# Part of a one-core mixer's weights split into high and low halves ahead of time and kept in DRAM, other remainders moved from GpSimd to VectorE, and the q, k norm multiplied from PSUM

## The chip, the cores and the metric

The kernel runs on one core of a Trainium2 chip. The metric is the device time of one execution in microseconds; the time before is the median of three runs. A core has TensorE (PE, with weight loads listed as PEld), VectorE (DVE), ScalarE (ACT), GpSimd (POOL) and SyncE (SP). DVE and ACT can read PSUM, the memory into which PE accumulates, in eight banks of 128x512 f32. SP here only issues DMAs, in the order of the program; POOL issues those DMAs that add to their target. Each engine works off its own instructions in order.

## The reference

One layer of a streaming encoder on x of 1024 x 1024, f32, in three residual steps:

```
h  = rmsnorm(x);  z = h @ w_in         # q, f, i, g (HGRN), q, k, v (band attention), two gates
oa = hgrn2(q, f, i, g)                 # 4 heads of 128, a recurrence over chunks of 64
ob = band_attention(q, k, v)           # 8 heads of 64, own chunk and the 8 before it
       # q and k go through head_rms first: t * rsqrt(mean(t*t over 64) + eps) * gain
x += (sigmoid(gate_a) * (oa @ w_branch_a) + sigmoid(gate_b) * (ob @ w_branch_b)) @ w_out
x += (silu(h2 @ w_gate) * (h2 @ w_up)) @ w_down          # h2 = rmsnorm(x)
x += sigmoid(h3 @ w_ple_gate) * (p @ w_ple_proj)         # h3 = rmsnorm(x)
```

## The kernel before

*Products in three passes.* Each f32 operand a is split into hi = a rounded to the type that PE multiplies at full rate, and lo = a - hi. A product is hi*hi + hi*lo + lo*hi (`gemm`). The split is a cast (hi) and a subtraction (lo, "the remainder"). Of a weight, ACT makes hi and mostly POOL makes lo.

*Order of the work.* The program is one long Python routine (`run`) that emits instructions; every engine keeps the emitted order (`order`, line 71). The stages are:

1. **units** (line 967): the first norm, the projections whose weights are combined before use (gates, HGRN's q, f, g), as twelve jobs (`JOBS`) of seven products each (`strassen`). While one job's products run, a generator `side` prepares the next job's weights: sums on DVE, casts on ACT, remainders on DVE and POOL (`strassen_weights`). Results go to DRAM.
2. **the HGRN heads 0 to 3** (`hgrn_mix`): chains of small DVE products, each level feeding small matmuls. They are woven (`weave`) with a stream of large products, `fill`: two gates (`gate_first`), v (`attn_v`), and the first part of q, k (`attn_in`). Each item of the stream is six 128x512 matmuls. Loads of each head's operands are issued by SP in the same emitted order (`head_load`, `head_late`, `near`).
3. **the attention** (`attention`): 32 steps of scores, softmax, transposes and products with v; between them, two items per step of the rest of `attn_in` and then of `branch_a` (oa @ w_branch_a). At steps 18, 19, 19 and 20 (`SPLITS`), `split_in` casts HGRN's output on ACT and makes its remainder on POOL.
4. **branches, out_proj, FFN, ple**: the rest, which the change does not touch but for one line.

*Weights of stages 2 and 3.* The list `worder` holds pieces of 128x1024 f32 (512 KB): two gates, four of v, eight of q and k (four for the first half of the heads, four for the second), then the branches'. `fetch` (line 166) takes the next one: it issues the load into one of two raw buffers (`RAW`) and puts a generator `cast` in the list `later`. `tick` advances everything in `later` by one step; `ticked` calls it after each item of the stream. So two to three items after the load, ACT casts the piece into one of four ring buffers (`RING`), and POOL makes the remainder right behind it. `got` hands out finished pieces.

*The norm of q and k* (`qk_norm`, line 652) is a generator in `later` too, one for each of 16 results of 128x512 in PSUM. In its first step it copies the result to SBUF (ACT in the heads, DVE in the attention) and squares it in PSUM; in the second DVE sums the squares, POOL takes the power -0.5 and multiplies the copy; three ticks later SP stores it. The attention loads it back (`qk_load`).

*POOL's other work there:* DMAs that add blocks of the weights of w_out and w_ffn_down in DRAM (`dma_sums`), issued at every odd step and at each pair of tiles of `branch_a`.

In the profile, line 73 stands for every instruction of DVE, ACT and POOL that goes through the ordering helper (`Pinned`), line 104 for matmuls, line 107 for transposes, line 99 for SP's DMAs. Tiles: `wr` raw weight, `wh` and `wl` its halves, `whi` and `wlo` halves in the units, `s` a 128x1024 slot, `m` a small tile, `pm` a PSUM bank, `t` a 128x512 scratch tile, `d` a block in DRAM, `in_...` an input.

Of the kernel before, what the change touches and what calls it, by code (L numbers as in the profile page):

```python
# [11 lines left out]
F32R = mybir.dt.float32r  # L12
U8 = mybir.dt.uint8
U32 = mybir.dt.uint32
AF = mybir.ActivationFunctionType
ALU = mybir.AluOpType
AX = mybir.AxisListType

P = 128
T = 1024  # L20
D = 1024
# [9 lines left out]
SLOTS = 32  # L31
LATE = 8
FIRST = 5
GROUPS = ((0, 1), (2,), (3,), (4,), (5,), (6, 7))
RING = 4
RAW = 2
# [9 lines left out]
def f32(ap):  # L46
    return ap.bitcast(F32)
# [28 lines left out]
class Trunk:  # L76
    def __init__(self, tc, d, out):
        self.tc, self.nc, self.d, self.out = tc, tc.nc, d, out
        self.V = Pinned(self, self.nc.vector, "dve")
        self.A = Pinned(self, self.nc.scalar, "act")  # L80
        self.G = Pinned(self, self.nc.gpsimd, "pool")
        self.n = self.turn = 0
        self.queue, self.calls = None, 0
        self.later = []
        self.by_turns = self.pinned = False
        self.ahead = 2
        self.done = set()
        self.prev = {}
# [77 lines left out]
    def fetch(self):  # L166

        if self.wnext < len(self.worder):
            hi, lo, raw, ap = self.unit()
            c = slice(0, ap.shape[1])  # L170
            self.load(raw[:, c], ap[:, c])

            def cast():
                yield
                yield
                self.A.copy(hi[:, c], raw[:, c])
                self.G.tensor_tensor(lo[:, c], raw[:, c], f32(hi[:, c]), ALU.subtract)
                self.wready.append((hi, lo))

            self.later.append(cast())  # L180

# [8 lines left out]
            yield got  # L190

    def got(self, n=1):
        while len(self.wready) < n:
            assert self.later
            self.tick()
        got, self.wready = self.wready[:n], self.wready[n:]
        return got

    def lazy(self, ws):
        for _ in range(4):  # L200
# [450 lines left out]

    def qk_norm(self, k, ps):

        late = self.stacks
        qk = self.small(HALF, tag="qk" if late else "bias", shape=(P, HALF if late else 640))[:, :HALF]
        (self.V.tensor_copy if late else self.A.copy)(qk, ps)
        self.A.activation(ps, ps, AF.Square)
        yield
        ss = self.small(8)
        heads = lambda t: t.rearrange("p (a d) -> p a d", d=64)  # L660
        self.V.tensor_reduce(ss, heads(ps[:, :]), axis=AX.X, op=ALU.add)
        b = k % 8
        self.V.tensor_scalar(ss, ss, 1.0 / 64, self.epsv[:, b:b + 1], ALU.mult, ALU.add)
        self.G.tensor_tensor(ss, ss, self.mhalf[:, 0:8], ALU.pow)
        self.G.tensor_tensor(heads(qk), heads(qk), ss[:, :].unsqueeze(2).to_broadcast([P, 8, 64]), ALU.mult)
        yield
        yield
        yield
        self.store(self.qk_at(k), qk)
# [199 lines left out]
    def split_in(self, raw):  # L869

        hi = self.slot(F32R)
        self.A.copy(hi, f32(raw[:, :]))
        self.G.tensor_tensor(raw, f32(raw[:, :]), f32(hi[:, :]), ALU.subtract)
        return hi, raw

    def split_half(self, src, half):
# [84 lines left out]
    def units(self, outs):  # L961

        V, A = self.V, self.A
        h0, h1 = slice(0, HALF), slice(HALF, T)
        self.gd = [self.spill() for _ in range(2 * KC)]
        self.gh = [self.spill() for _ in range(4)]
        self.vd = [self.spill() for _ in range(4)]
        self.hd = [[] for _ in range(4)]
        self.kept = []
        self.t32, self.t1, self.xs = [], [], []  # L970

        ws = self.weights(4, ahead=0)
        for k in range(4):
            xe = self.slot()
            if k < 2:
                xo = self.slot()
                self.mix_load(k, xe, [xo[:, :HALF], xo[:, HALF:]], xo)
            else:
                self.mix_load(k, xe, [self.stmp(), self.stmp()])
        self.strassen_load()  # L980
        side = chain(*[self.mix_sums(k) for k in range(4)])

        def rest():
            more = self.units_first()
            next(more)
            yield
            yield from self.mix_last()
            for i in (2, 3, 0, 1):
                self.head_out(0, *head, i // 2, i % 2, outs[i])
                yield  # L990
            yield from more

        for blks in ((0, 1), (2,), (3,), (4,), (5,), (6,), (7,)):
            pss = []
            for j, _ in enumerate(self.tokens(ws, blks, pss)):
                if blks[0] == 0 and j == 3:
                    self.norm_sums()
                next(side, None)
            if blks[0] == 4:
                self.strassen_load()  # L1000
            for b, ps in zip(blks, pss):
                t = self.stmp()
                A.activation(t, ps, AF.Copy, scale=self.r[:, b:b + 1])
                to = self.vd[b // 2][:, b % 2 * HALF:b % 2 * HALF + HALF]
                if b >= 4:
                    to = bass.AP(to.tensor, to.offset + (TURN - 1) * T, [[TURN * T, P // TURN], [-T, TURN], [1, HALF]])
                self.store(to, t)
            if blks[0] == 0:
                self.norm_rows()
            if blks[0] == 4:  # L1010
                drain(side)
                head = self.slot(), self.slot()
                side = rest()
        drain(side)
        u, t = self.u, self.t32
        cut = lambda pair, h: [x[:, h] for x in pair]
        four = range(4)
        self.sops = [
            [cut(u[2 * k + 1], h1) for k in four], [cut(t[k], h1) for k in four],
            [cut(self.t1[k // 2], slice(k % 2 * HALF, k % 2 * HALF + HALF)) for k in four], [cut(t[k], h0) for k in four],  # L1020
            [cut(u[2 * k], h1) for k in four], [cut(u[2 * k + 1], h0) for k in four], [cut(u[2 * k], h0) for k in four]]
        pack = self.head_pack(0, *head)
        for n, (kind, i) in enumerate(JOBS):

            def side():
                more = self.strassen_weights() if n + 1 < len(JOBS) else self.mix_first()
                next(more, None)
                if n + 2 < len(JOBS):
                    self.strassen_load()
                yield  # L1030
                for _ in more:
                    next(pack, None)
                    yield
                drain(pack)

            if kind == "head":
                q, f = self.slot(), self.slot()
                done = lambda c, half, ps: self.head_out(i, q, f, c, half, ps)
            elif kind == "gate":
                done = lambda c, half, ps: self.gate_done(self.gd[i + c], half, ps, AF.Sigmoid)  # L1040
            else:
                done = lambda c, half, ps: self.gate_done(self.gh[i + c], half, ps, AF.Silu)
            self.strassen(done, side(), early=n == 0)
            if kind == "head":
                pack = self.head_pack(i, q, f)
        self.gate_keep()
        for k in range(4):
            hi, lo = self.u[2 * k + 1]
            c = C_MIX + 2 * k + 1
            g = self.cols[:, c:c + 1]  # L1050
            A.activation(hi[:, h0], self.xb[k], AF.Copy, scale=g)
            V.scalar_tensor_tensor(lo[:, h0], self.xb[k], g, f32(hi[:, h0]), ALU.mult, ALU.subtract)
        self.A.activation(self.warm, self.warm, AF.Sigmoid)

    def units_first(self):
# [24 lines left out]
        self.wrest(G, cut(a12, h1), r2[:, h1])  # L1080
        yield
        self.sready = (a11, cut(s21, h0), cut(s21, h1), s3, cut(a12, h0), cut(a12, h1), s4)

    def mix_first(self):
        self.fetch()
# [61 lines left out]
    def branches(self):  # L1147
# [4 lines left out]
        drain(self.feed)  # L1152
        while self.later:
            self.tick()
        for dd in range(4):
            (w,) = self.weights()
            next(self.adds, None)
# [933 lines left out]
    def run(self):  # L2091
# [17 lines left out]
        with ExitStack() as es:  # L2109
            self.cp = es.enter_context(tc.tile_pool(name="const", bufs=1))  # L2110
            self.wp = es.enter_context(tc.tile_pool(name="weights", bufs=RING))
            self.rp = es.enter_context(tc.tile_pool(name="raw", bufs=RAW))
            self.dp = es.enter_context(tc.tile_pool(name="spill", bufs=4 * KC + 11 * STEPS + 56, space=bass.MemoryType.DRAM))
            self.sp = es.enter_context(tc.tile_pool(name="slots", bufs=SLOTS))
            self.tp = Small(tc, es, SMALL)
            self.pp = es.enter_context(tc.tile_pool(name="psum", bufs=8, space=PS))
# [60 lines left out]
class Small:  # L2177
# [5 lines left out]
    def tile(self, shape, dt, tag, name):  # L2183
        return self.pools[tag].tile(shape, dt, tag=tag, name=name)


def drain(stream):
    while True:
        try:
            next(stream)  # L2190
        except StopIteration as e:
            return e.value
# [125 lines left out]
```

## Time and profile before

| what | us |
|---|---|
| median of three runs (1553.53 to 1553.84) | 1553.71 |
| the profiled execution | 1554.34 |
| its span, first to last instruction | 1552.5 |
| PE busy (98%) | 1518.9 |
| DVE busy (72%) | 1122.6 |
| ACT busy (43%) | 665.0 |
| POOL busy (44%) | 683.2 |

The units take the span up to about 306 us, the heads with their stream to about 470, the attention to about 680; from there to the end it is branches, output, FFN and the last step. The mean granted clock of PE is 0.993 of full speed. In the views, "idle before <-" names what released an engine from a wait; a row of the timeline gives start, duration, engine, line, operation, output<-inputs and count.

### The profile page before, as it was taken

How to read it: one execution, taken by the hardware profiler on the slowest of the kernel's cores; microseconds unless marked ns; L12 is line 12 of the kernel's file. 1: busy time of each engine (PE TensorE's matmuls, PEld its weight loads, DVE VectorE, ACT ScalarE, POOL GpSimd, SP SyncE). 2: the span in 40 equal slices, each digit the busy share in tenths (PEclk: the TensorE clock that was granted, in tenths of full speed). 3: DMA queues.
4: the chain of work that ended last, by engine and by line, in shares of the span. 5: the costliest groups of instructions: out<-in, count | busy, mean ns of one | idle time of the engine just before them, and what ended most of it. 6: DMA issues, size and time to landing. Idle time of an engine off the chain costs nothing.

```text
span 1552.5 us, 20777 instructions
## 1 busy us (share of the span) xinstructions
PE 1518.9 (98%) x7680; PEld 1251.0 (81%) x7680; DVE 1122.6 (72%) x1594; ACT 665.0 (43%) x1119; POOL 683.2 (44%) x383
## 2 busy tenths in 40 slices
PE   8999999999898998999999999999999999999998
PEld 6888888878786886888888888888888888888886
DVE  5776777476776766746998877777777767756668
ACT  6633333344335665741557322222222234446552
POOL 4233333320235426237221666665555544545546
PEclk9999999999999998999999999999999999999999
DMA  5543444466537768558245234443333288875425
GB/s 202 193 169 103 143 143 156 176 239 213 181 118 249 178 188 256 139 154 259 90 163 216 97 115 125 128 125 113 107 103 104 94 310 302 288 273 186 129 95 203
DMA packets 101940, 264.95 MB, mean 171 GB/s; under 512 B 10576, under 2 KB 15440, under 8 KB 101328
## 3 DMA queue, kind: packets, MB, share of 16 engines
q1 hardware_dynamic: 95296, 247.90, 46.1%
q0 software_dynamic: 6400, 15.73, 6.1%
q8 instruction: 60, 0.98, 0.3%
q14 instruction: 40, 0.33, 0.1%
q10 hardware_dynamic: 144, 0.02, 0.0%
HBM read 197.28 MB, written 97.78 MB: 190 GB/s over the span
## 4 chain that ended last, share of the span: by engine, by line
PE 83%; DVE 8%; DMA 3%; issue 2%; POOL 2%; ACT 2%; SPq 0%; DVEq 0%; POOLq 0%; ACTq 0%
PE pm L104 81%; DVE s L73 6%; PE pm L107 3%; POOL s L73 1%; DMA wr<-in_qk 1%; ACT s L73 1%; DVE m L73 1%; DMA wr<-in_bb 1%; POOL wl L73 0%; DVE wl L152 0%; ACT wh L144 0%; DMA s<-in_x 0%; POOL wl L152 0%; DMA wr<-in_ow 0%; DMA m<-d 0%
## 5 line engine op out<-in xcount | busy, mean ns | idle before, releaser
L104 PE MATMUL pm<-s,whi 128*128 128x512 f32 x1904 | 586.4, 389 | 0.0
L104 PE MATMUL pm<-s,wh 128*128 128x512 f32 (+1 forms) x1456 | 455.1, 393 | 13.9 <-POOL s L73 6.8
L104 PEld LDWEIGHTS pm<-s,whi 128*128 128x128 f32 x1904 | 357.4, 188 | 74.2
L104 PE MATMUL pm<-s,wlo 128*128 128x512 f32 x952 | 370.6, 389 | 0.5 <-DVE wlo L73 0.5
L73 DVE TENSOR_TENSOR s<-s,s 128x512 f32<-128x512 f32 (+3 forms) x240 | 296.5, 1265 | 58.7 <-ACT s L73 42.5
L104 PEld LDWEIGHTS pm<-s,wh 128*128 128x128 f32 x1456 | 271.9, 189 | 72.7 <-POOL s L73 7.6
L104 PE MATMUL pm<-s,wl 128*128 128x512 f32 (+1 forms) x728 | 284.3, 391 | 0.5 <-POOL wl L152 0.5
L152 POOL TENSOR_TENSOR wl<-wr,wh 128x1024 fp32r<-128x1024 f32 (+3 forms) x71 | 177.0, 2496 | 218.7 <-ACT wh L144 215.3
L73 DVE TENSOR_TENSOR t<-pm,t 128x512 f32<-128x512 f32 x168 | 115.7, 689 | 147.3 <-PE pm L104 124.9
L104 PEld LDWEIGHTS pm<-s,wlo 128*128 128x128 f32 x952 | 178.7, 188 | 38.1 <-DVE wlo L73 1.2
L104 PE MATMUL pm<-wh,s 128*128 128x512 f32 x512 | 181.7, 410 | 0.0
L73 POOL TENSOR_TENSOR wlo<-q,whi 128x512 fp32r<-128x512 f32 x66 | 105.1, 1593 | 164.2 <-ACT whi L73 87.8
L73 POOL TENSOR_TENSOR wlo<-wr,whi 128x1024 fp32r<-128x1024 f32 (+1 forms) x67 | 139.8, 2093 | 68.4 <-ACT whi L73 59.3
L104 PEld LDWEIGHTS pm<-s,wl 128*128 128x128 f32 x728 | 137.5, 189 | 29.7 <-POOL wl L152 1.2
L144 ACT CAST wh<-wr 128x1024 fp32r<-128x1024 f32 (+2 forms) x82 | 81.2, 992 | 154.6 <-PE pm L104 41.2
L73 ACT CAST s<-s 128x1024 fp32r<-128x1024 f32 (+1 forms) x104 | 98.7, 970 | 61.7 <-DMA s<-d 27.0
L73 ACT CAST whi<-q 128x512 fp32r<-128x512 f32 (+1 forms) x99 | 75.0, 758 | 107.0 <-PE pm L104 87.1
L73 POOL TENSOR_TENSOR s<-t,rb 128x512 f32<-128x512 f32 x44 | 71.2, 1619 | 99.3 <-ACT t L73 99.3
L104 PEld LDWEIGHTS pm<-wh,s 128*128 128x128 f32 x512 | 97.5, 190 | 19.0
L104 PE MATMUL pm<-wl,s 128*128 128x512 f32 x256 | 101.0, 394 | 0.0
L73 POOL TENSOR_TENSOR wl<-wr,wh 128x1024 fp32r<-128x1024 f32 x25 | 61.0, 2444 | 90.3 <-ACT wh L73 83.5
L73 ACT ACTIVATE t<-s 128x512 f32<-128x512 f32 x44 | 27.8, 632 | 158.6 <-DVE s L73 154.6
(149 smaller groups left out, 1809.3 us busy)
## 6 DMA issues: line engine op xcount, KB each, us to landing
s<-d SPq DMA_DIRECT2D x81, 512.0 KB, 6.5
d<-s SPq DMA_DIRECT2D x87, 256.0 KB, 2.3
wr<-d SPq DMA_DIRECT2D x36, 512.0 KB, 3.4
d<-s SPq DMA_DIRECT2D x30, 512.0 KB, 4.7
d<-t SPq DMA_DIRECT2D x54, 256.0 KB, 2.1
wr<-in_sz SPq DMA_DIRECT2D x24, 512.0 KB, 6.1
wr<-in_sg SPq DMA_DIRECT2D x22, 512.0 KB, 4.0
wr<-in_su SPq DMA_DIRECT2D x22, 512.0 KB, 4.2
```

The source lines that it names most:

```text
L73: return lambda *a, **k: self.trunk.order(op(*a, **k), self.key)
L104: return self.order(self.nc.tensor.matmul(*a, **k))
L107: return self.order(self.nc.tensor.transpose(*a, **k))
L144: self.nc.scalar.copy(hi[:, c], raw[:, c])
L152: rest.tensor_tensor(lo[:, c], raw[:, c], f32(hi[:, c]), ALU.subtract)
```

## The change

- **Pieces prepared in the units.** In jobs 1, 2, 9 and 10, `side` runs a new generator `presplit` for two pieces each: the four of v and the first four of q, k. It loads the piece into a slot, ACT casts it, POOL makes the remainder, and both halves are stored to DRAM (two blocks of 512 KB). `fetch` then loads both halves of such a piece straight into ring buffers, with no cast, and marks it ready at once.
- **Other remainders.** The two gates, the last four of q, k and the pieces of the branches that `fetch` takes are still cast by ACT, but DVE makes the remainder, one tick after the cast. A list `order_w` with ready marks takes the place of `wready` until `branches` begins. `split_in` also leaves its remainder to DVE, at the next tick.
- **The norm.** `qk_norm` no longer copies the result: ACT squares from PSUM into SBUF, DVE sums, POOL takes the power, and a tick later DVE multiplies straight from PSUM into the tile that is stored. The PSUM bank is held until then.
- The pool of DRAM blocks grows by 16.

```diff
+PRE = {1: (0, 1), 2: (2, 3), 9: (4, 5), 10: (6, 7)}
...
     def fetch(self):
         if self.wnext < len(self.worder):
+            parts = self.parts.get(self.wnext)
+            if parts:
+                self.wnext += 1
+                w = self.wtiles(D)
+                for t, src in zip(w, parts):
+                    self.load(f32(t[:, :]), src)
+                self.order_w.append([w, True])
+                return
             hi, lo, raw, ap = self.unit()
...
                 yield
                 yield
                 self.A.copy(hi[:, c], raw[:, c])
-                self.G.tensor_tensor(lo[:, c], raw[:, c], f32(hi[:, c]), ALU.subtract)
-                self.wready.append((hi, lo))
+                yield
+                self.V.tensor_tensor(lo[:, c], raw[:, c], f32(hi[:, c]), ALU.subtract)
+                entry[1] = True
+
+            entry = [(hi, lo), False]
+            self.order_w.append(entry)
...
     def got(self, n=1):
-        while len(self.wready) < n:
-            assert self.later
+        while not all(ready for _, ready in self.order_w[:n]):
             self.tick()
-        got, self.wready = self.wready[:n], self.wready[n:]
-        return got
+        got, self.order_w = self.order_w[:n], self.order_w[n:]
...
     def qk_norm(self, k, ps):
-        late = self.stacks
-        qk = self.small(HALF, tag="qk" if late else "bias", shape=(P, HALF if late else 640))[:, :HALF]
-        (self.V.tensor_copy if late else self.A.copy)(qk, ps)
-        self.A.activation(ps, ps, AF.Square)
+        tile = lambda: self.small(HALF, tag="qk" if self.stacks else "bias", shape=(P, HALF if self.stacks else 640))[:, :HALF]
+        heads = lambda t: t.rearrange("p (a d) -> p a d", d=64)
+        sq = tile()
+        self.A.activation(sq, ps, AF.Square)
         yield
         ss = self.small(8)
-        heads = lambda t: t.rearrange("p (a d) -> p a d", d=64)
-        self.V.tensor_reduce(ss, heads(ps[:, :]), axis=AX.X, op=ALU.add)
         b = k % 8
+        self.V.tensor_reduce(ss, heads(sq), axis=AX.X, op=ALU.add)
         self.V.tensor_scalar(ss, ss, 1.0 / 64, self.epsv[:, b:b + 1], ALU.mult, ALU.add)
         self.G.tensor_tensor(ss, ss, self.mhalf[:, 0:8], ALU.pow)
-        self.G.tensor_tensor(heads(qk), heads(qk), ss[:, :].unsqueeze(2).to_broadcast([P, 8, 64]), ALU.mult)
-        yield
+        yield
+        qk = tile()
+        self.V.tensor_tensor(heads(qk), heads(ps[:, :]), ss[:, :].unsqueeze(2).to_broadcast([P, 8, 64]), ALU.mult)
         yield
         yield
         self.store(self.qk_at(k), qk)
...
     def split_in(self, raw):
         hi = self.slot(F32R)
         self.A.copy(hi, f32(raw[:, :]))
-        self.G.tensor_tensor(raw, f32(raw[:, :]), f32(hi[:, :]), ALU.subtract)
+        def rest():
+            self.V.tensor_tensor(raw, f32(raw[:, :]), f32(hi[:, :]), ALU.subtract)
+            yield
+        self.later.append(rest())
         return hi, raw
...
+                pre = [self.presplit(j) for j in PRE.get(n, ())]
                 yield
                 for _ in more:
                     next(pack, None)
+                    for p in pre:
+                        next(p, None)
                     yield
                 drain(pack)
+                for p in pre:
+                    drain(p)
...
+    def presplit(self, j):
+        k = 6 + len(FIRSTS) + j
+        raw, hi = self.slot(F32R), self.slot(F32R)
+        self.load(f32(raw[:, :]), self.worder[k])
+        yield
+        yield
+        self.A.copy(hi, f32(raw[:, :]))
+        self.G.tensor_tensor(raw, f32(raw[:, :]), f32(hi[:, :]), ALU.subtract)
+        yield
+        self.parts[k] = [self.spill() for _ in range(2)]
+        for to, t in zip(self.parts[k], (hi, raw)):
+            self.store(to, f32(t[:, :]))
...
     def branches(self):
         while self.later:
             self.tick()
+        self.wready = [w for w, _ in self.order_w]
```

More of the change, by code (lines that the diff above doesn't have):

```diff
@@ L84, in __init__ @@
         self.later = []
+        self.parts, self.order_w = {}, []
         self.by_turns = self.pinned = False
@@ L192, in got @@
     def got(self, n=1):
-        while len(self.wready) < n:
-            assert self.later
+        while not all(ready for _, ready in self.order_w[:n]):
             self.tick()
-        got, self.wready = self.wready[:n], self.wready[n:]
-        return got
+        got, self.order_w = self.order_w[:n], self.order_w[n:]
+        assert len(got) == n
+        return [w for w, _ in got]
     def lazy(self, ws):
@@ L2112, in run @@
             self.rp = es.enter_context(tc.tile_pool(name="raw", bufs=RAW))
-            self.dp = es.enter_context(tc.tile_pool(name="spill", bufs=4 * KC + 11 * STEPS + 56, space=bass.MemoryType.DRAM))
+            self.dp = es.enter_context(tc.tile_pool(name="spill", bufs=4 * KC + 11 * STEPS + 72, space=bass.MemoryType.DRAM))
             self.sp = es.enter_context(tc.tile_pool(name="slots", bufs=SLOTS))
```

## The prediction

> **What bounds the kernel now.** I read the page's head first: TensorE (PE) is busy 98% of the span.
>
> ```profile
> span 1552.5 us, 20777 instructions
> PE 1518.9 (98%) x7680; PEld 1251.0 (81%) x7680; DVE 1122.6 (72%) x1594; ACT 665.0 (43%) x1119; POOL 683.2 (44%) x383
> ```
>
> So a change that removes no matmul can win only what PE idles, 1552.5 - 1518.9 = 33.6 us, and what it runs at a lower clock. The second view, busy time by stretch (width first, then PE, PEld, DVE, ACT, POOL, the granted clock, DMA share, GB/s), says where that is. The first row is a units job (`strassen`) that gets new work; the six others are the mixer.
>
> ```profile
> 98.00:117.00 19.00, 19.00 (x86) 15.73 (x85) 14.16 (x20) 7.52 (x12) 8.17 (x4) 1.00 0.70 250
> 300.00:395.00 95.00, 94.11 (x578) 78.93 (x577) 63.74 (x110) 36.86 (x77) 13.09 (x8) 1.00 0.65 222
> 395.00:422.00 27.00, 22.50 (x151) 18.47 (x150) 24.11 (x33) 12.51 (x28) 10.00 (x5) 0.94 0.71 209
> 422.00:475.00 53.00, 51.31 (x343) 43.45 (x342) 35.99 (x73) 17.16 (x40) 17.76 (x14) 1.00 0.32 103
> 475.00:510.00 35.00, 30.40 (x177) 22.20 (x178) 22.06 (x69) 22.88 (x66) 20.82 (x13) 0.95 0.85 267
> 510.00:578.00 68.00, 67.73 (x585) 55.91 (x583) 48.78 (x177) 46.03 (x114) 21.26 (x18) 1.00 0.72 191
> 578.00:612.00 34.00, 27.20 (x140) 19.38 (x136) 19.72 (x47) 19.75 (x55) 23.41 (x15) 0.85 0.81 241
> ```
>
> PE idles 0.89, 4.50, 1.69, 4.60, 0.27 and 6.80 us in the six mixer rows, 18.75 us together, and three of them show a clock below 1. The same view on the long holes and what follows them:
>
> ```profile
> 345.60:346.70 1.10, 0.41 (x2) 0.00 (x0) 1.10 (x2) 0.00 (x0) 0.53 (x1) 1.00 0.00 0
> 399.90:402.10 2.20, 0.76 (x4) 0.29 (x2) 2.20 (x3) 0.67 (x2) 0.95 (x1) 1.00 0.27 28
> 414.60:418.10 3.50, 0.48 (x3) 0.08 (x2) 3.50 (x5) 0.00 (x0) 2.18 (x1) 1.00 1.09 278
> 418.60:422.00 3.40, 3.40 (x17) 2.81 (x15) 2.35 (x5) 0.20 (x1) 0.00 (x0) 0.50 0.95 302
> 483.80:486.60 2.80, 0.42 (x2) 0.00 (x0) 1.69 (x4) 2.80 (x11) 2.33 (x1) 1.00 1.07 345
> 486.90:490.20 3.30, 3.30 (x12) 2.27 (x12) 2.25 (x9) 1.82 (x8) 2.38 (x1) 0.50 1.08 284
> 497.30:499.00 1.70, 0.42 (x3) 0.23 (x3) 1.70 (x5) 1.18 (x3) 0.00 (x0) 1.00 1.05 236
> 589.60:592.50 2.90, 0.46 (x3) 0.03 (x2) 1.51 (x3) 2.15 (x8) 2.90 (x3) 1.00 1.03 420
> 592.70:596.00 3.30, 3.30 (x12) 2.11 (x12) 3.30 (x3) 0.48 (x1) 2.03 (x1) 0.50 1.08 325
> 598.20:603.00 4.80, 0.52 (x2) 0.19 (x1) 4.69 (x7) 3.15 (x8) 3.40 (x3) 0.99 0.52 126
> 603.00:609.70 6.70, 6.62 (x31) 4.81 (x32) 2.60 (x8) 1.16 (x4) 6.54 (x7) 0.50 0.47 110
> ```
>
> The holes cost 0.69, 1.44, 3.02, 2.38, 1.28, 2.44 and 4.28 us of PE. Four are followed by a stretch at clock 0.50 (3.4, 3.3, 3.3, 6.7 us), in which half the time is lost: 1.7, 1.65, 1.65, 3.35. Grouped: **heads** (before 422) 0.69 + 1.44 + 3.02 + 1.7 = 6.85; **weights of q, k** (483 to 499) 2.38 + 1.65 + 1.28 = 5.3; **splits** (589 to 610) 2.44 + 1.65 + 4.28 + 3.35 = 11.7. Together 23.9 us; the 1.69 us between 422 and 475 and the 0.27 after 510 come in pieces well below these, and I leave them as they are.
>
> The third view, the timeline, names the cause. Heads:
>
> ```profile
> 395.93 1.28 DVE L73 TENSOR_TENSOR s<-s,s 128x512 f32<-128x512 f32 x2
> 398.46 2.39 POOL L73 TENSOR_TENSOR wl<-wr,wh 128x1024 fp32r<-128x1024 f32 x1 [2.94 <-PE pm L104]
> 398.83 3.17 DVE L73 TENSOR_TENSOR s<-s,s 128x512 f32<-128x512 f32 x2
> ...
> 412.08 4.70 POOL L73 TENSOR_TENSOR wl<-wr,wh 128x1024 fp32r<-128x1024 f32 x2 [3.83 <-ACT wh L73]
> 412.12 2.40 DVE L73 TENSOR_TENSOR s<-s 128x32 f32<-128x32 f32 x1
> ```
>
> The same pair of VectorE (DVE) products takes 1.28 us alone and 3.17 beside POOL's remainder of a weight; a small 128x32 product takes 2.40 beside the next two. DVE stands still while POOL works on SBUF, and PE, which waits for these products, stands with it.
>
> Weights of q and k, and splits:
>
> ```profile
> 479.09 0.29 DVE L73 TENSOR_SCALAR s<-s,m 128x128 f32<-128x128 f32 x1
> ...
> 483.02 1.05 ACT L73 CAST wh<-wr 128x1024 fp32r<-128x1024 f32 x1 [3.37 <-DMA wr<-in_qk]
> ...
> 485.24 1.34 DVE L73 TENSOR_SCALAR s<-s,m 128x128 f32<-128x128 f32 x1
> 486.52 3.21 SPq L99 DMA_DIRECT2D wr<-in_qk  x2
> ...
> 588.98 1.07 POOL L73 DMA_DIRECT2D d<-in_wq  x1
> 589.58 5.14 POOL L73 TENSOR_TENSOR s<-s,s 128x1024 fp32r<-128x1024 f32 x2
> 591.31 3.58 DVE L73 TENSOR_SCALAR s<-s,m 128x256 f32<-128x256 f32 x1
> 599.60 1.06 POOL L73 DMA_DIRECT2D d<-in_wq  x1 [4.87 <-DMA m<-d]
> ```
>
> At 483 there are two causes: ACT stood 3.37 us for a weight that had not landed, and then a softmax scaling took 1.34 us beside POOL's remainder instead of the 0.29 of the step before. At 589 and 598 PE waits directly for POOL's remainders of the HGRN output (`split_in`), the last of which stood 4.87 us behind an accumulating DMA.
>
> **The change, part by part.** Prices of what replaces POOL's work:
>
> ```profile
> L73 DVE TENSOR_TENSOR s<-s,s 128x1024 fp32r<-128x1024 f32 x2 | 2.4, 1222 | 2.5 <-ACT s L73 2.5
> L73 POOL TENSOR_TENSOR m<-m,mhalf 128x8 f32<-128x8 f32 x16 | 27.4, 1712 | 58.2 <-DVE m L73 48.7 <-DMA m<-in_bias 9.4
> L73 POOL TENSOR_TENSOR m<-m,m 128x512 f32<-128x512 f32 x16 | 16.9, 1056 | 1.3
> L73 DVE COPY m<-pm 128x512 f32<-128x512 f32 x12 | 7.9, 680 | 0.0
> L73 DVE TENSOR_TENSOR s<-pm,s 128x512 f32<-128x512 f32 x64 | 42.8, 683 | 29.4 <-PE pm L104 26.7 <-DMA s<-d 2.0
> ```
>
> The rows are, in this order: a remainder on DVE (1.22 us, against 2.39 to 2.57 on POOL above), the powers of the norms on POOL, the product of the norms on POOL, the copy that the norms make on DVE, and a DVE product that reads PSUM, the nearest row to the new one. DVE's row for the remainder is from the start, where POOL is idle; beside POOL it would be held as the products above are.
>
> *Pieces prepared in the units.* Jobs 1, 2, 9 and 10 each get two pieces: two loads, two ACT casts (1.05), two POOL remainders (2.39) and four stores of 512 KB. POOL goes from 8.17 to 12.9 of 19 us, ACT from 7.52 to 9.6, traffic by 3 MB in 19 us (about 160 GB/s) from 250 to some 410, just under the 420 that a row above shows. DVE, at 14.16, can be held 4.8 us more by POOL and then fills its 19. PE is full in these rows and the weights are made a job ahead, so I charge 0.5 us for all four jobs; the ends are 0 and 4. Later those eight pieces need no cast and no remainder, so nothing of POOL's stands beside heads 0 to 3 but the powers: all 6.85 us of the heads go.
>
> *Their fetch.* Two loads go straight into ring tiles, so SP must wait until PE has let the old piece go. Everything behind it on SP's queue waits too.
>
> ```profile
> 373.25 1.04 SPq L99 DMA_DIRECT2D wr<-in_qk  x2
> ...
> 384.11 11.39 SPq L99 DMA_DIRECT2D s<-d  x8
> ```
>
> SP took the first two q, k pieces at 373, some 20 us ahead of PE. Now it stands there until the first v piece is done, at about 395, and the loads of head 2's v and head 3's operands follow at 398 or later. From then 2 MB of pieces, 0.5 of copies, 0.75 of `m<-d` and 2.5 of `s<-d` go out, 5.75 MB; at 222/0.65 = 340 GB/s that is 17 us, to about 412. By the program's order v is used after all seven levels of the head, which by the heads' share (four heads between 330 and 475, 36 us each) is about 25 us into head 2, at 418, an estimate. I charge 0.5 us; the ends are 0 and 5.
>
> *Remainders on DVE, one piece later.* The last four q, k pieces and the output weights keep their casts. At 485.24 POOL costs DVE 1.05 us (1.34 - 0.29); a remainder of 1.22 now stands in DVE's own queue, so that trade is even. ACT's 3.37 us wait for the weight stays. The load at 486.52 started as POOL let the raw buffer go; it now waits for a DVE remainder a tick later, perhaps 1.5 us. Of the 5.3 us I take 1.0; the ends are -1.5 and 5.3.
>
> *`split_in` on DVE.* The four remainders cost DVE 4 x 1.22 = 4.9 us there, instead of four on POOL of some 2.57 (5.14/2). DVE had 19.72 of 34 us busy in that row, at least 3 of it held by POOL (the scaling of 3.58), so it has room over the whole row but not at the steps where three splits meet. I leave 2.5 us for that. The last weight norms fall into the same place (next part).
>
> *The norm from PSUM.* Per block an ACT or DVE copy goes (0.68 on DVE, twelve times) and POOL's product goes (1.06, sixteen times), and a DVE product from PSUM comes (0.68, sixteen times). DVE's load grows by 4 x 0.68 = 2.7 us over 160 and loses what POOL's product held it; that is even. What is new is that DVE now waits for POOL's power (1.71) a tick after issuing its input, and the bank is held that long. A tick holds at least six matmuls, 6 x 19.00/86 = 1.3 us, and half a step of the attention's own work, so a single power is nearly always done in time; at the last pair, powers stand behind two accumulating DMAs that were 10.6 us apart (588.98, 599.60), and DVE would stand 2 to 4 us. I leave 2.0 us of idling and 1.2 for the slow clock. Of the splits' 11.7 I take 11.7 - 2.5 - 3.2 = 6.0; the ends are 0 and 11.7.
>
> The row at 483.80 idles 2.38 us and the next one runs at clock 0.50, so a hole that is left at 2 to 3 us still costs clock. The Trainium skill (TensorE: Matmul & The Clock Gate, "Part 1: The HAM clock gate") puts the fall to half clock at an idle window of about 3.4 us; the trace has it after less, and the measurement decides. By the page the 1.2 us just charged would not arise, and the sum below would come to 1540.0.
>
> **Sum.** 6.85 - 0.5 - 0.5 + 1.0 + 6.0 = 12.85, of which I take off 0.35 for the extra norms' bank time, 12.5. The profiled run took 1554.34 us (span 1552.5), 0.63 over the median of 1553.71. 1554.34 - 12.5 - 0.63 = 1541.2.
>
> **Rivals.**
> *All holes close.* DVE takes the remainders in its pauses and the powers come in time: 6.85 + 4 + 9.5 less 0.5 is 19.85, 1533.9. Four of the 5.3 and 9.5 of the 11.7 is what is left when only ACT's wait and one short hole remain. For it: DVE is busy 90.5 of 137 us after 475. Against: steps are in order, and its pauses are not where the remainders are due.
> *DVE becomes the bound of the attention.* Only the heads gain; the moved 1.22 us pieces open as much as they close: 6.85 - 2 is 5, 1548.7. For it: at 483 to 499 idle PE follows DVE delays of about a microsecond.
> *Slower: DVE parks behind the powers.* Sixteen norms; each makes DVE wait for up to 1.71 us, or 3.4 at a pair, with PE behind it. It decides from a mean stall of 0.8 us per norm, where 16 x 0.8 = 12.8 eats the forecast's gain. At the full 1.71 it is 27 us, 1568; I price it at 1.2 per norm, 19 less 12.5, 1560. Against: a tick lies between.
> *No change*: the loads that SP holds reach head 2 late and cost what the heads win (6.85), and the rest stays even: about 1553. It needs DMA at under three quarters of the 340 GB/s above.
>
> **How the numbers follow.** Forecast 0.50 (own range 1537 to 1546), all holes 0.17, DVE-bound 0.18, no change 0.06, slower 0.09. The likeliest gives 1541.2. From 1534.5 to 1550.5 no more than 2 in 10 is left out: slower, most of no change, and the lower part of all holes. 0.2% is 3.1 us, about what a measurement of this kernel can tell from no change: faster 0.85, same 0.06, slower 0.09.
>
> **What would show it.** Heads: no 2.4 us POOL remainder between 330 and 470, the 128x32 product at about 0.2 us, clock 1.00 from 395 to 422. Units: PE still 19.00 of 19 in the job's row. Splits: 1.22 us DVE remainders and one hole of 2 to 4 us, DVE's, behind a power. Wrong would be: holes in head 2 released by `m<-d` or `s<-d` loads, a hole at each norm, or PE below 19 in the jobs.

## The result, and the profile after

The changed kernel took 1543.04 us (median, 1541.62 to 1545.48) beside 1553.62 us of the kernel before on the same chip: a ratio of 0.9937, with a 95% interval of 0.9919 to 0.9954. That is 10.6 us less; 12.5 were forecast. On another chip the same pair stood at 1541.67 to 1552.08, ratio 0.9932 (0.9918 to 0.9947). The profiled execution took 1541.62 us, 12.7 less than the one of before, its span 13.0 less; it is the fastest of the four runs, so the rows below add up to more than the 10.6 us of the medians.

The head of the page after:

```profile
span 1539.5 us, 20816 instructions
PE 1515.0 (98%) x7680; PEld 1249.8 (81%) x7680; DVE 1131.2 (73%) x1616; ACT 662.6 (43%) x1115; POOL 633.9 (41%) x349
```

PE idles 24.5 us instead of 33.6. Busy time by stretch of the kernel after (columns as before: width, PE, PEld, DVE, ACT, POOL, clock, DMA share, GB/s); the first row lies in the units, where pieces are prepared, the next six are the stretches of the prediction, then a new hole and what follows it, and what follows the hole that is left at the splits:

```profile
117.00:136.00 19.00, 18.72 (x83) 15.16 (x82) 16.52 (x13) 10.30 (x15) 14.92 (x7) 1.00 0.81 293
300.00:395.00 95.00, 94.86 (x583) 80.02 (x582) 62.38 (x113) 34.09 (x74) 4.03 (x4) 1.00 0.63 223
395.00:422.00 27.00, 25.42 (x175) 20.58 (x174) 19.16 (x36) 9.89 (x26) 0.00 (x0) 1.00 0.95 348
422.00:475.00 53.00, 48.24 (x310) 41.14 (x308) 34.56 (x72) 14.61 (x35) 12.64 (x9) 0.94 0.48 156
475.00:510.00 35.00, 33.77 (x234) 25.81 (x234) 25.08 (x88) 25.86 (x74) 8.86 (x6) 1.00 0.98 286
510.00:578.00 68.00, 67.64 (x563) 55.79 (x562) 48.31 (x171) 44.68 (x118) 15.46 (x12) 1.00 0.71 184
578.00:612.00 34.00, 31.60 (x213) 23.87 (x211) 26.64 (x79) 25.70 (x67) 9.90 (x8) 0.95 0.99 295
436.30:440.90 4.60, 0.38 (x2) 0.00 (x0) 2.76 (x6) 0.47 (x1) 2.77 (x2) 0.89 0.20 77
440.90:447.70 6.80, 6.55 (x23) 5.69 (x24) 4.74 (x9) 3.34 (x11) 0.00 (x0) 0.57 0.33 102
592.20:596.50 4.30, 4.30 (x28) 3.25 (x29) 3.09 (x8) 2.41 (x6) 2.99 (x2) 0.65 1.08 285
```

What a stretch loses is its width less PE busy, plus its width times what the clock lacks. Against the rows of before:

| stretch | lost before (idle + clock) | lost after | gain | forecast |
|---|---|---|---|---|
| heads, 300 to 422 | 5.4 + 1.6 | 1.7 + 0 | 5.3 | 6.35 with the loads' 0.5 |
| rest of head 3, 422 to 475 | 1.7 + 0 | 4.8 + 3.2 | -6.2 | 0 |
| weights of q, k, 475 to 510 | 4.6 + 1.75 | 1.2 + 0 | 5.1 | 1.0 |
| 510 to 578 | 0.3 | 0.4 | -0.1 | 0 |
| splits, 578 to 612 | 6.8 + 5.1 | 2.4 + 1.7 | 7.8 | 6.0 |

The sum is 11.9 of the span's 13.0; the other 1.1 lies in pieces outside these rows or in the rounding of the clock, and was not traced. So the total came out near the forecast by luck, by errors of opposite sign: a new hole of head 3, and more gain than forecast at the weights of q, k and at the splits.

The new hole is the first line of PE's waits between 300 and 680 us of the kernel after (what PE waited for: us in all, times, longest); in before the first was POOL's remainders with 6.8 us:

```profile
PE pm L106 <- ACT m L74: 4.8, 2, 4.5
PE pm L106 <- DVE s L74: 2.4, 2, 2.1
...
PE pm L106 <- DMA wlo<-d: 0.8, 1, 0.8
PE pm L106 <- DMA whi<-d: 0.4, 1, 0.4
```

The timeline of the kernel after, first the place of the third large hole of before, then the new hole, then the last pair of splits:

```profile
410.11 0.18 DVE L74 TENSOR_TENSOR s<-s 128x32 f32<-128x32 f32 x1
...
435.84 3.23 POOL L74 TENSOR_TENSOR m<-m,mhalf 128x8 f32<-128x8 f32 x2 [4.14 <-DVE m L74]
...
437.51 0.69 DVE L74 TENSOR_TENSOR m<-pm,m 128x512 f32<-128x512 f32 x1 [0.89 <-POOL m L74]
...
439.11 0.69 DVE L74 TENSOR_TENSOR m<-pm,m 128x512 f32<-128x512 f32 x1 [0.91 <-POOL m L74]
439.72 1.28 DVE L74 TENSOR_TENSOR s<-s,s 128x512 f32<-128x512 f32 x2
...
440.43 0.62 ACT L74 COPY m<-s 128x512 f32<-128x512 f32 x1 [7.05 <-DVE s L74]
...
441.15 1.20 PE L106 MATMUL pm<-s,m 128*128 128x128 f32 x4 [4.47 <-ACT m L74]
...
588.46 1.06 ACT L74 CAST s<-s 128x1024 fp32r<-128x1024 f32 x1
...
590.00 0.68 DVE L74 TENSOR_REDUCE m<-m 128x8 f32<-128x512 f32 x1
...
590.54 4.65 POOL L74 TENSOR_TENSOR m<-m,mhalf 128x8 f32<-128x8 f32 x2
...
590.85 1.22 DVE L74 TENSOR_TENSOR s<-s,s 128x1024 fp32r<-128x1024 f32 x1
...
592.12 0.50 PE L106 MATMUL pm<-s,wh 128*128 128x512 f32 x1 [2.05 <-DVE s L74]
```

At 410 the small product takes 0.18 us where it took 2.40. At 436 read upwards from PE: it waited for ACT's copy, ACT for DVE's pair of products at 439.72, and that pair stood behind two norm products, each of which waited for its power. The engine named in the waits view (ACT) is only the last link; the first is POOL's pair of powers, 3.23 us. At 590 the hole is that of DVE's own remainder: ACT's cast ended at 589.52, but DVE first made the sums of the last pair of norms (the second at 590.00, then a small step) and came to the remainder at 590.85. The groups of the same kernel give DVE's whole wait for the powers (busy and mean ns of one, then idle before):

```profile
L74 DVE TENSOR_TENSOR wl<-wr,wh 128x1024 fp32r<-128x1024 f32 x12 | 14.5, 1218 | 0.0
...
L74 DVE TENSOR_TENSOR m<-pm,m 128x512 f32<-128x512 f32 x16 | 11.1, 691 | 8.7 <-POOL m L74 8.6
```

DVE's remainder of a ring piece costs the forecast 1.22 us; the sixteen norm products wait 8.6 us, 0.54 each.

### The profile page after: what moved, and what is told of

It is laid out like the page before. It is cut to its first block, busy times and chain, and to the rows that moved or that the text cites. A ratio compares the mean times of both kernels' runs of the same rounds, so it can differ in the third digit from the quotient of the medians.

```text
span 1539.5 us, 20816 instructions
## 1 busy us (share of the span) xinstructions
PE 1515.0 (98%) x7680; PEld 1249.8 (81%) x7680; DVE 1131.2 (73%) x1616; ACT 662.6 (43%) x1115; POOL 633.9 (41%) x349
## 4 chain that ended last, share of the span: by engine, by line
PE 91%; DVE 4%; DMA 2%; issue 1%; ACT 1%; POOL 1%; SPq 0%; POOLq 0%; ACTq 0%; DVEq 0%
PE pm L106 89%; PE pm L109 2%; DVE s L74 2%; DVE m L74 1%; POOL m L74 1%; DMA s<-d 1%; DMA wlo<-d 0%; DMA wr<-in_qk 0%; ACT s L74 0%; DMA s<-in_x 0%; ACT m L74 0%; DVE q L74 0%; DVE s L391 0%; SPq L101 0%; DVE wl L74 0%
## 5 line engine op out<-in xcount | busy, mean ns | idle before, releaser
L74 DVE TENSOR_TENSOR s<-s,s 128x512 f32<-128x512 f32 (+3 forms) x246 | 292.5, 1219 | 65.4 <-ACT s L74 49.2
L74 POOL TENSOR_TENSOR wlo<-wr,whi 128x1024 fp32r<-128x1024 f32 (+1 forms) x67 | 144.0, 2157 | 67.1 <-ACT whi L74 58.0
L74 ACT CAST s<-s 128x1024 fp32r<-128x1024 f32 (+1 forms) x112 | 106.9, 976 | 68.7 <-DMA s<-d 29.2
L74 POOL TENSOR_TENSOR m<-m,mhalf 128x8 f32<-128x8 f32 (+1 forms) x24 | 36.8, 1604 | 218.3 <-DVE m L74 207.9
L106 PE MATMUL pm<-whi,s 128*128 128x512 f32 x256 | 93.2, 414 | 0.4 <-DMA whi<-d 0.4
L106 PE MATMUL pm<-wh,s 128*128 128x512 f32 x256 | 88.1, 403 | 0.0
L74 DVE TENSOR_TENSOR s<-s,pm 128x512 f32<-128x512 f32 x72 | 45.9, 682 | 34.3 <-PE pm L106 34.3
```

The source lines that it names most:

```text
L74: return lambda *a, **k: self.trunk.order(op(*a, **k), self.key)
L106: return self.order(self.nc.tensor.matmul(*a, **k))
```

## The experiments

Four questions were open: what releases the hole at 436; what each part of the change is worth by itself; whether the pieces of the units are needed; and what is left after that. Each ratio is to the kernel before on the same chip, with its 95% interval.

**The changed kernel again**, for the reference of the next three.

> The changed kernel again, beside the three variants on one chip. Expected 1541 to 1545 us, some 10.5 us under before, with the same one long hole of PE at 436 us (4.5 us, then 6.8 us at half clock).

Measured: 1541.67 us, 0.9932 (0.9918 to 0.9947). Its trace differs from the first mainly at one place, the late halves of a q, k piece in head 2 (timeline, then the stretch behind it):

```profile
416.03 0.50 PE L106 MATMUL pm<-whi,s 128*128 128x512 f32 x1 [0.59 <-DMA whi<-d]
...
418.62 0.50 PE L106 MATMUL pm<-wlo,s 128*128 128x512 f32 x1 [2.09 <-DMA wlo<-d]
```

```profile
419.00:423.00 4.00, 4.00 (x14) 3.23 (x13) 0.00 (x0) 0.59 (x1) 0.00 (x0) 0.57 1.03 395
```

The waits for the two halves were 0.4 and 0.8 us in the first profile and 0.6 and 2.1 here, and of these two only here the clock falls behind them (0.57 over 4 us). So the heads (300 to 422) lose 4.6 us in this profile where the first lost 1.7, and gain 2.4 over before instead of 5.3. The loads' price varies from one run to the next.

**One tick more before the norm's product.**

```diff
         self.G.tensor_tensor(ss, ss, self.mhalf[:, 0:8], ALU.pow)
         yield
+        yield
         qk = tile()
...
         yield
-        yield
         self.store(self.qk_at(k), qk)
```

> One tick more between the power and the product of the norm. Theory (DVE stands in its order behind the two powers of a pair, POOL's 3.2 us): the hole at 436 us falls from 4.5 to under 1.5 us and its slow clock goes, 5 to 8 us faster than the changed kernel, 1535 to 1538. Rival (the hole comes of the PSUM bank that is held longer): it is held a tick longer still, so the hole stays or grows, 1543 to 1547. Rival (late loads in SP's queue): no change.

Measured: 1535.40 us, 0.9893 (0.9881 to 0.9906), 6.1 us under the kernel after by ratio. Its timeline at the same place, and its group of norm products:

```profile
438.14 3.46 POOL L74 TENSOR_TENSOR m<-m,mhalf 128x8 f32<-128x8 f32 x2 [4.14 <-DVE m L74]
...
438.82 1.28 DVE L74 TENSOR_TENSOR s<-s,s 128x512 f32<-128x512 f32 x2
...
440.25 1.02 PE L106 MATMUL pm<-s,m 128*128 128x128 f32 x7 [1.28 <-ACT m L74]
```

```profile
L74 DVE TENSOR_TENSOR m<-pm,m 128x512 f32<-128x512 f32 x16 | 10.6, 683 | 2.2 <-POOL m L74 2.2
```

DVE's chain now goes before the norm products, PE's hole shrinks from 4.47 to 1.28 us, and DVE's waits for powers from 8.6 to 2.2. The bank is held a tick longer and the loads are no earlier (PE waits 1.1 and 1.4 us for the halves), so neither of these was the cause: it was the order on DVE, with the head's chain behind two products that wait for their powers. That is shown. The 3.19 us by which the hole shrank are the two waits of the kernel after, 0.89 and 0.91 us, and the two products themselves, 0.69 each: the waits are a little over half of it.

**The old norm in the changed kernel** (`qk_norm` as before, the rest as after).

```diff
-        self.A.activation(sq, ps, AF.Square)
+        (self.V.tensor_copy if late else self.A.copy)(qk, ps)
+        self.A.activation(ps, ps, AF.Square)
...
-        self.V.tensor_tensor(heads(qk), heads(ps[:, :]), ss..., ALU.mult)
+        self.G.tensor_tensor(heads(qk), heads(qk), ss..., ALU.mult)
```

> The norm alone as before (copy, POOL's product), all else changed. Theory of the powers: the hole at 436 us goes back to the 1.3 us that it had before and its slow clock goes (-6.5), while POOL's products of 1.06 us hold DVE again (+1 to +3): 1537 to 1541. If the new norm is worth something on the whole: 1544 to 1548.

Measured: 1544.51 us, 0.9951 (0.9933 to 0.9968). Its stretches:

```profile
422.00:475.00 53.00, 51.30 (x345) 43.24 (x343) 36.87 (x78) 19.47 (x46) 18.01 (x15) 1.00 0.48 151
475.00:510.00 35.00, 30.39 (x186) 22.21 (x186) 21.15 (x73) 23.06 (x67) 11.81 (x9) 0.95 0.90 270
```

and, of its timeline, the old norm's copies:

```profile
493.31 1.28 DVE L74 COPY m<-pm 128x512 f32<-128x512 f32 x2
```

The hole at 436 is gone (51.30 of 53, clock 1.00), but 475 to 510 is back at 4.6 us of idling and clock 0.95. So the gain at the weights of q and k, which the prediction put down to the remainders, needs the new norm too. The two copies of a pair stand on DVE between a weight's remainder and the step that PE waits for, 2.40 us at 495.20; the kernel after has 1.00 us at 494.84, without them. In sum the new norm is worth little inside this change: 2.9 us by ratio, but the intervals of 0.9951 and 0.9932 overlap.

**No pieces in the units.**

```diff
-PRE = {1: (0, 1), 2: (2, 3), 9: (4, 5), 10: (6, 7)}
+PRE = {}
```

> No pieces prepared in the units; v and the first q, k are cast in the heads, with DVE's remainder. Theory A (the heads' 6.85 us came of POOL holding DVE): the holes at 345, 400 and 415 stay small, as DVE makes the remainders, 0 to 3 us slower than the changed kernel. Theory B (the work has to leave the heads): they return as DVE's own time, 5 to 7 us slower, 1548 to 1550. The waits for the loads of the halves at 416 us (1.2 us) go in both.

Measured: 1541.17 us, 0.9928 (0.9916 to 0.9940), the same as with them. All pieces of v, q and k now have their remainder on DVE. Its timeline:

```profile
408.88 1.22 DVE L74 TENSOR_TENSOR wl<-wr,wh 128x1024 fp32r<-128x1024 f32 x1 [1.61 <-ACT wh L74]
...
410.02 1.29 DVE L74 TENSOR_TENSOR s<-s,s 128x512 f32<-128x512 f32 x2
...
411.36 0.70 PE L106 MATMUL pm<-s,s 128*32 128x32 f32 x32 [2.14 <-DVE s L74]
```

One hole, at 409, where the remainder waits for its cast, stands in place of the late halves at 416 to 418.

**The splits back on POOL** (`split_in`'s remainder at once on POOL).

```diff
-        def rest():
-            self.V.tensor_tensor(raw, f32(raw[:, :]), f32(hi[:, :]), ALU.subtract)
-            yield
-        self.later.append(rest())
+        self.G.tensor_tensor(raw, f32(raw[:, :]), f32(hi[:, :]), ALU.subtract)
```

> split_in's remainder on POOL at once, as before; all else as changed. Theory (the prediction's term for the splits, 6.0 us, is what this move brings): the two holes of PE that POOL's remainders made return (2.4 and 4.3 us before, each with a slow clock behind it), 4 to 8 us slower than the changed kernel, 1546 to 1550. Rival (POOL, rid of its other work there, is in time anyway): within 2 us of the changed kernel.

Measured: 1547.93 us, 0.9967 (0.9956 to 0.9979), 5.4 us over the kernel after by ratio. PE's two waits, of its timeline:

```profile
589.89 0.50 PE L106 MATMUL pm<-s,wh 128*128 128x512 f32 x1 [1.35 <-POOL s L74]
...
598.69 0.79 PE L106 MATMUL pm<-s,wh 128*128 128x512 f32 x1 [4.19 <-POOL s L74]
```

**The ring pieces' remainders back on POOL**, right behind the cast.

```diff
                 self.A.copy(hi[:, c], raw[:, c])
-                yield
-                self.V.tensor_tensor(lo[:, c], raw[:, c], f32(hi[:, c]), ALU.subtract)
+                self.G.tensor_tensor(lo[:, c], raw[:, c], f32(hi[:, c]), ALU.subtract)
                 entry[1] = True
```

> The remainders of the pieces that are still cast go to POOL, right behind the cast, as before; all else as changed, so the heads have none of them. Theory (the trade of 1.05 held against 1.22 own is even, and the prediction gave it 1.0): 0 to 2.5 us slower than the changed kernel, the holes at 483 to 497 us as before.

Measured: 1548.55 us, 0.9975 (0.9964 to 0.9985), 6.7 us over: far more than expected. Its timeline:

```profile
497.71 2.38 POOL L74 TENSOR_TENSOR wl<-wr,wh 128x1024 fp32r<-128x1024 f32 x1 [1.95 <-ACT wh L74]
498.01 2.11 DVE L74 TENSOR_SCALAR m<-m,m 128x8 f32<-128x8 f32 x1
...
500.26 3.27 POOL L74 TENSOR_TENSOR m<-m,mhalf 128x8 f32<-128x8 f32 x2 [0.17 <-DVE m L74]
...
500.74 0.23 DVE L74 TENSOR_SCALAR m<-m,m 128x8 f32<-128x8 f32 x1
...
501.96 0.69 DVE L74 TENSOR_TENSOR m<-pm,m 128x512 f32<-128x512 f32 x1 [0.41 <-POOL m L74]
502.71 0.44 PE L109 MATMUL pm<-eye,m 128*128 128x128 f32 x2 [2.62 <-DVE m L74]
```

The remainder hurts twice: it holds the small DVE step in front of the power (2.11 us, and 0.23 for the next one), and the powers stand behind it on POOL. In the old norm POOL's own product followed a power; in the new one DVE waits for the power, and PE for DVE. This edit also takes out the tick between cast and remainder, as the one on the splits does. POOL's remainder with that tick was not run, so these times do not tell the engine from the tick; that POOL's work holds DVE is read from the rows themselves.

**Both: no pieces, and remainders on POOL.**

> No pieces prepared in the units and all remainders of fetched pieces on POOL, as before; only split_in and the norm as changed. With the run without pieces (1541.2) and the one with POOL's remainders this fills the square. Theory (POOL beside the heads is what costs, and either half of the change is enough to cure it): the heads' holes of 0.7, 1.4 and 3.0 us and the slow clock return, 5 to 8 us slower than the changed kernel, 1547 to 1550. Rival (the heads gained nothing; the splits are all of the gain): 1541 to 1543.

Measured: 1549.82 us, 0.9982 (0.9973 to 0.9991). The held product of the kernel before is back (timeline):

```profile
411.67 4.69 POOL L74 TENSOR_TENSOR wl<-wr,wh 128x1024 fp32r<-128x1024 f32 x2 [3.83 <-ACT wh L74]
411.71 2.40 DVE L74 TENSOR_TENSOR s<-s 128x32 f32<-128x32 f32 x1
```

With and without the pieces the ratios are 0.9932 and 0.9928 with DVE's remainders, 0.9975 and 0.9982 with POOL's: the move of the remainders is worth 0.0043 to 0.0054, the pieces between -0.0004 and 0.0007, within the intervals.

**The pieces alone** (the kernel after with the cast's and the splits' remainders on POOL and the old norm; the edits are those above).

> The pieces prepared in the units alone; the other remainders, split_in and the norm as before. Theory (the heads' 6.85 us go with any cure of POOL there, less the late loads at 416 us, 1 to 4 us): 2 to 6 us faster than before. Rival (the pieces are worth nothing by themselves, since without them the changed kernel was as fast): within 1.5 us of before.

Measured: 1550.80 us, 0.9988 (0.9978 to 0.9997), 1.9 us faster than before. In its profile the heads lose 4.5 us, where the kernel before loses 7.0; PE waits 1.3 and 1.1 us for the late halves.

**The norm alone** (the kernel before with the new `qk_norm`).

> The norm alone as changed, on the kernel before. Theory (DVE in its order behind POOL's powers, and those behind POOL's remainders): the hole of 4.5 us in head 3 appears with its slow clock, others where powers stand behind remainders of weights or splits, 4 to 9 us slower than before. Rival (the product off POOL frees DVE): 1 to 3 us faster.

Measured: 1554.82 us, 1.0017 (1.0008 to 1.0026), 2.6 us slower; slower as expected, by less. Its timeline and three of its stretches:

```profile
443.26 2.05 PE L104 MATMUL pm<-s,m 128*128 128x128 f32 x8 [4.47 <-ACT m L73]
```

```profile
422.00:475.00 53.00, 48.24 (x319) 41.64 (x318) 34.14 (x72) 15.29 (x37) 12.64 (x9) 0.97 0.33 108
475.00:510.00 35.00, 30.98 (x184) 22.91 (x183) 22.80 (x71) 22.19 (x65) 17.75 (x10) 0.95 0.89 260
578.00:612.00 34.00, 28.67 (x150) 20.87 (x147) 19.10 (x46) 19.42 (x55) 21.62 (x12) 0.80 0.88 244
```

The hole of head 3 comes with the norm and has the same 4.47 us. Idling at 475 and 578 is 0.6 and 1.5 us less than before, where POOL's products are gone; the clock at 578 is lower (0.80 for 0.85).

**Splits one step earlier, with the longer tick.**

```diff
-SPLITS = (18, 19, 19, 20)
+SPLITS = (17, 18, 18, 19)
```

> The extra tick of the norm, and the four splits a step earlier (17, 18, 18, 19). Theory (the hole at 590 us is the last split's cast and remainder standing in ACT's and DVE's order behind the last pair of norms): the hole of 2.05 us and its slow clock go, 2 to 4 us faster than the kernel with the tick alone (1535.4), 1531.5 to 1533.5. Rival (the hole is DVE being full in these steps): it moves a step earlier, within 1 us of 1535.4.

Measured: 1533.98 us, 0.9877 (0.9864 to 0.9890), 2.5 us under the version with the tick alone, by ratios of two chips whose intervals overlap a little. Its stretch at the splits, which idled 2.4 us at clock 0.95:

```profile
578.00:612.00 34.00, 34.00 (x265) 27.28 (x264) 27.81 (x93) 24.94 (x67) 7.93 (x7) 1.00 1.02 302
```

**That, and SP's copies out of head 2.** SP issued copies of weight blocks between the loads of head 2.

```diff
-            if m in (2, 8, 32):
+            if m in (2, 8, 32) and h != 2:
                 next(self.copies, None)
```

> The kernel with the extra tick and the earlier splits, and without the three copies in DRAM (0.5 MB each) that SP issues in head 2, which come later instead. Theory (the hole at 415 us is traffic: 7 MB in 20 us behind SP's wait): the waits for the halves there (1.6 us) go, ratio to before 0.001 to 0.003 under that of the kernel without this (0.9877). Rival (SP issues the loads too late whatever else moves): no change.

Measured: 1529.93 us, 0.9855 (0.9841 to 0.9869). The stretch with the late halves has 0.38 us of idling left, and PE has no wait for a half in it:

```profile
395.00:422.00 27.00, 26.62 (x187) 21.98 (x186) 18.94 (x36) 10.48 (x27) 0.00 (x0) 1.00 0.95 338
```

**The tick and the splits, and no pieces.**

> The kernel with the extra tick and the earlier splits, without pieces prepared in the units. Theory (DVE's remainders cost the heads one hole at 409 us of 2.1 us and its slow clock, the prepared pieces cost one at 415 us of 1.6): 0 to 3 us slower than with them, ratio 0.9877 to 0.990. If the pieces are worth nothing: 0.986 to 0.988.

Measured: 1529.72 us, 0.9857 (0.9844 to 0.9870). Its heads have the hole of the version without pieces (timeline):

```profile
411.03 0.70 PE L106 MATMUL pm<-s,s 128*32 128x32 f32 x32 [2.15 <-DVE s L74]
```

So it is no slower without the pieces. Both versions beat the kernel before by 1.4% and the changed kernel by 0.8%. The one with the copies moved and the pieces omitted was not run.

## Why the prediction came out right, and where its steps were wrong

Four of the kernels form a ladder in which each adds one part, so their ratios price the parts: the norm alone 1.0017 (2.6 us lost); with `split_in` on DVE 0.9982 (5.4 gained); with the ring pieces' remainders on DVE 0.9928 (8.4 gained); with the pieces 0.9932 (none). Putting the splits back on POOL in the full change cost 5.4 as well. The first rung, the second, and the last two were measured on three chips, each with its own runs of before. A part's price depends on what is there already: the norm loses 2.6 us alone, and taken out of the full change it costs 2.9, though in intervals that overlap.

- **Cause, right.** POOL's work on SBUF held DVE, and PE stood with it: 2.40 us against 0.18 for the same product, coming back beside POOL's remainders when these go back to POOL.
- **Heads, wrong in what earns it, and near in size in two profiles of eight.** The prediction gave the 6.85 us to the pieces, because "nothing of POOL's stands beside heads 0 to 3 but the powers". DVE's remainders without pieces give the same time, and the pieces alone 1.9 us. One step that failed is that a DVE remainder at the heads was not priced: it is 1.22 us with no idle before it in the groups above, and without the pieces leaves one hole of 2.14 us. As to size, the rows of the eight versions and runs that have the pieces, with SP's copies where they were, gain 5.3, 2.4, 2.6, 3.2, 1.1, 2.2, 2.5 and 5.3 us at the heads; 6.35 were forecast. What is missing is mainly the price of the late halves.
- **Units, right.** PE loses 0.28 us in the stretch where POOL has 14.92 us of 19, and nothing there in the second profile; the charge was 0.5 for four jobs. But the work was added to the wrong row: the pieces' remainders run at 117.8 and 134.7, in stretches that had 6.24 us of POOL and 110 GB/s at 117 to 136 before, not the 8.17 and 250 of 98 to 117. So traffic rose to 293 GB/s, not 410.
- **Fetch and SP's order, too small.** Charged 0.5, ends 0 and 5. SP stood until 393.3 and came to the head's operands at 399.9, as foretold (395 and 398). But the prediction looked at those operands: its 418 is the time at which head 2 uses its v, and by its own shares (head 2 from 402, 25 us in) that would be 427. No such load held PE there. The late ones were the halves of a q, k piece (the last v piece was loaded at 333), which SP issued behind the operands, at 409.3 and 410.6. They cost waits of 1.2 us in the first profile, and 2.7 with a slow clock in the second. Taking SP's copies out of the way removed the waits and went with 3.4 us by ratio, in intervals that overlap slightly; whether the copies' place in the queue or their traffic did it (395 GB/s at that place) was not told apart.
- **Weights of q and k, too small.** Taken 1.0, gained 5.1. The rows of 475 to 510 lose 6.35 us before, 5.8 with the norm alone, 6.4 with DVE's remainders and the old norm, 4.8 with the new norm and POOL's remainders, and 1.2 with both. So the step that failed is the one that priced the remainders and the norm separately and called the copy and product of the old norm even. ACT's wait of 3.37 us for the first of these weights, which "stays" by the prediction, is gone (its cast at 480.03 waits for no load); with the norm alone it is gone too and the stretch still loses 5.8, so this wait was not all that cost PE. Beyond the copies shown above, the interplay was not traced.
- **Splits, right in size, in part by luck.** Taken 6.0, gained 7.8 in the profile and 5.4 by ratio. The hole that the prediction left at the last pair of norms is there, 2.05 us for 2.0 and 1.7 of slow clock for 1.2, but not with powers "behind two accumulating DMAs": PE waits for DVE's remainder, which stood behind the pair's sums. With the longer tick, splits a step earlier close it.
- **The norm: right mechanism, wrong place.** "At the last pair" should have been the first pair, in head 3, where the prediction left 422 to 475 as it was. The step that failed is "A tick holds at least six matmuls ... and half a step of the attention's own work". The first and the last of the groups (`GROUPS`) hold two blocks each, so their norms come as a pair, and its powers take 3.23 us. A tick holds some of DVE's other work only if the head emits any: DVE's queue has none between the pair's sums and its products at 437.51, so the head's next DVE chain goes behind both. It cost 6.2 us in the profile, and one tick took back 6.1.
- **The rivals.** The slower one was the right mechanism below its deciding point: 0.54 us per norm, where 0.8 was needed. Alone on the kernel before it does decide, 1.0017. "DVE becomes the bound" falls, since DVE's remainders earn 8.4 us. "All holes close", at 1533.9, is about what the two edits of waiting and order gave (1533.98). "No change" had a right mechanism too, late loads behind SP's wait, at a part of its price and with other loads than it named.

The row at 592.20 shows clock 0.65 over 4.3 us behind a hole of 2.05 us, so the slow clock again came after less than the window of about 3.4 us that the Trainium skill states (TensorE: Matmul & The Clock Gate, "Part 1: The HAM clock gate"). By the measurement the charge for it stands.

## What to carry to other kernels

Where two engines hold each other up in SBUF and one of them feeds PE, give it the shared work itself: 1.22 us in its own queue cost less than 2.4 us of being held. But when a step on a third engine then lies between two steps of the feeding engine, put enough of that engine's other work between them, and look for the place where two such steps meet; here that one line was worth 6.1 us. Price the parts by a ladder, and in more than one order: the part that took the most code, weights prepared ahead, was worth 1.9 us alone and nothing on top of the rest, and the norm cost 2.6 us alone and none in the full change.

## What the runs showed of the hardware

- POOL's remainder holds small DVE steps as well as products: a 128x8 `TENSOR_SCALAR` took 2.11 us beside it and 0.23 three microseconds later, beside a power. POOL's power on 128x8 did not hold larger ones either: a pair of two-input DVE products ran in 1.28 us inside a pair of powers of 3.46 us, as fast as alone. The Trainium skill (SBUF — State Buffer, "SBUF: two separate sides") calls the pair of ports that the two engines share "an exclusive lock, not a bandwidth split", held for the whole instruction, where DVE has two SBUF inputs or runs in a 2-port mode. The remainders agree with that; the powers show no such hold.
- The same hole of 4.47 us was followed by different losses of clock: in the stretch of 53 us the clock was 0.94 in the first profile of the change, and 0.97 with the norm alone. The length of shorter waits did not settle it either. Behind waits of 0.4 and 0.8 us for the two halves there was no loss; behind 0.8 and 0.8, with the old norm, the clock was 0.65 over the next 3 us. One hole of 2.14 us (no pieces) went with a clock of 0.94 over its stretch of 27 us, and one of 2.15 (no pieces, with the tick and the earlier splits) with 1.00.
- A pair of powers took 3.23 to 3.91 us elsewhere in the kernel after, and 4.65 at 590.54, where DVE's remainder ran beside it. Whether DVE held POOL there was not tested.
